# An SSD chunk loop with its products turned over: diagonal and skip on VectorE, gate on GpSimd, features kept transposed

## The chip, the cores and the metric

One core of one Trainium2 chip. The metric is the device time of one execution in microseconds (us). Times below are of single executions; the median is over three.

## The reference

Two layers over 1024 latent rows and 256 context rows, width 1024: windowed attention, then a bidirectional Mamba-2 SSD mixer, and a final RMSNorm. The change lies in the mixer. Per group of heads (8 groups of 4 heads of 64, state size 128) and per chunk of 128 rows it needs, cut to what matters:

```
a_cs   = cumsum(dt * A)                        # per head, forward or backward
states = einsum(B, exp(a_last - a_cs), x*dt)   # one state per chunk, then a scan over chunks
cb     = einsum('bcqgn,bcsgn->bcqsg', C, B)
y_diag = einsum(cb, exp(a_cs[q]-a_cs[s]) where s<=q, x*dt)
y_off  = einsum(C, h_prev, exp(a_cs))
y      = y_f + y_b + d_skip * x                # both directions, and the skip
u      = rms_normalize(y * silu(z))            # over the 256 columns of a group
out    = (u * norm_w) @ w_out
```

The latent scans start from the states that the context rows leave behind.

## The kernel before, in words

All large products run in split form: an f32 operand is taken apart into a high and a low part (hi is a cast, lo the difference), and three products hi*hi, hi*lo, lo*hi are summed in PSUM. The small products of the SSD part run in plain f32, each of which shows in the trace as two passes.

Attention comes first (up to about 690 us), then its output projection and the set-up of the decay rates (`dt_setup`, `dt_chain`, L914 to L1029). `ssd` (L1193) then loops over the 8 groups. For each group `front` (L1048) makes, in this order, B (tile bT), two halves of x, C (cT) and the gate z: projections on TensorE (L1143 for the context's 256 rows, L1152 for the 1024 latent rows, L1177 for z), a 5-tap convolution (`taps`, L1038 on VectorE), a silu, and transposes back to natural layout (`natural`, L1085, L1088). In L1177 the 128 rows of a chunk are stationary and 256 columns of the weight move, so that z comes out with rows on partitions; L1185 and L1188 make its silu.

`states` (L1223) walks the context's four chunk states and then the backward ones of the latent chunks: a weighting on GpSimd (L1213), a product (L1236), a decay on GpSimd (L1218) and a sum on VectorE (L1248). It is a generator, and `tick` advances it by one step, three times per chunk, once the group's x is finished; what is left runs at the end of the group.

`slot` (L1276) does one chunk of the current group, and between its steps `fill` runs pieces of the next group's `front`:

- L1282 makes C.B for the chunk (tile pcb), L1284 and L1285 the products with the forward and backward states (po: rows on partitions, two directions of 256 columns);
- L1286 multiplies the decays M, four heads of 128x128, with pcb; L1290 to L1293 advance the forward state (L1291 on TensorE);
- L1295 scales po by exp(a_cs), a per-row factor from the table `eacs`;
- L1300 takes the diagonal of pcb, L1302 makes the per-row skip factor sk, L1306 multiplies x by it on GpSimd, L1307 and L1308 sum the parts on GpSimd;
- L1311 is the diagonal product, four heads, M stationary and x moving with 64 columns; L1320 adds it, L1321 multiplies by the gate (both VectorE);
- L1323 squares and sums along the row (ScalarE), L1324 makes the power -1/2 (GpSimd), L1329 scales the row (ScalarE);
- `decays` (L1267) makes M for the next chunk: L1265 on GpSimd, L1270 on VectorE, four exponentials L1272 on ScalarE; `load_rows` (L1257) loads its rows two chunks ahead;
- the tail, run in the next chunk, transposes y twice (L1341), multiplies by norm_w on eviction (L1342) and stores the features (L1343).

During the last group `ssd_out` (L1433) runs instead of a front: it loads the features back (L1517), casts and splits them (L1529, L1526), casts and splits the weights (L1503, L1507) and runs the output projection (L1571, later L223 to L225).

Order: instructions are emitted by these generators under a planner (`Queue`, L64): FRONT and OUT are the planned costs of a front and of the output projection, SEGS the shares of the fill in a chunk. A scheduler then orders each engine's instructions along a simulated timeline, so that the emitted order is a priority. Each engine, and SyncE's DMA queue, then works in the order that it was given. PSUM has eight banks: pj2 (two tiles of two banks) for the projections, psX (three) for the slot's products, psD (one) for context and states.

## Time and profile before

| | us |
|---|---|
| median of three (1813.79, 1818.71, 1822.03) | 1818.71 |
| the profiled execution | 1818.37 |
| its span, first to last instruction | 1816.6 |
| start of the first chunk, and of the last group's first chunk | 857.2, 1593.9 |
| last product of the output projection's sweeps (L1571) | 1749.0 |

The page of the profile gives the busy time of each engine, with matmul ends that are modelled: TensorE's times overlap, so spacing between starts is the better price. The profile's other views used here are: stages (busy time per engine in a stretch of time), groups of instructions (count, busy sum, mean of one, idle time before), waits (who waited for whom: total, times, longest), the chain (the work that ended last), and the timeline of single instructions. PE is TensorE, DVE is VectorE, ACT is ScalarE, POOL is GpSimd, SP is SyncE, and SPq is its DMA queue.

### The profile page before, as it was taken

What the parts mean: (1) busy time and instruction counts of PE and PEld (TensorE: products, weight loads), DVE (VectorE), ACT (ScalarE), POOL (GpSimd) and SP (SyncE); (2) the same over time, 40 slices, a digit from 0 to 9 for tenths busy, and PEclk for the clock granted to TensorE, in tenths of its full rate; (3) what the DMA queues carried; (4) which work ended last, traced back from release to release, by engine and by line L of the source; (5) the groups of instructions that cost most, each with busy time, mean ns of one, the idle gap of its engine ahead of it and who ended that gap; (6) DMA issues with size and microseconds to landing.
All of it is one profiled execution on the core that took longest, in us unless ns stands there. A gap on an engine that the chain in (4) does not pass through costs nothing.

```text
span 1816.6 us, 29129 instructions
## 1 busy us (share of the span) xinstructions
PE 1749.0 (96%) x10379; PEld 1500.2 (83%) x10379; DVE 1166.0 (64%) x2125; ACT 869.9 (48%) x1895; POOL 811.1 (45%) x1074
## 2 busy tenths in 40 slices
PE   6999998999999899999999999999999999999997
PEld 3797767788889687778898898989889898988886
DVE  3563536786787766675766748567675857766643
ACT  3521235677788766352444434344353434544522
POOL 2441127554456465303454544646454454644311
PEclk9999999999999999999999999999999999999998
DMA  8768865543345445311322323323332322655542
GB/s 296 285 156 255 261 192 138 119 116 99 99 117 132 118 133 195 112 42 52 86 68 79 93 69 88 82 71 79 78 93 78 82 79 74 188 163 179 163 137 70
DMA packets 209393, 227.89 MB, mean 125 GB/s; under 512 B 16096, under 2 KB 149088, under 8 KB 208224
## 3 DMA queue, kind: packets, MB, share of 16 engines
q1 hardware_dynamic: 175184, 207.38, 38.1%
q0 software_dynamic: 34064, 18.65, 5.6%
q8 instruction: 82, 1.34, 0.3%
q14 instruction: 63, 0.52, 0.1%
HBM read 191.14 MB, written 35.13 MB: 125 GB/s over the span
## 4 chain that ended last, share of the span: by engine, by line
PE 83%; DVE 5%; ACT 4%; DMA 4%; issue 3%; POOL 0%; SPq 0%; DVEq 0%; ACTq 0%; POOLq 0%
PE pj L1152 17%; PE pj L1177 10%; PE pj L1571 7%; PE pj L223 6%; PE pj L225 6%; PE pj L224 6%; PE psD L1143 3%; PE pt L694 3%; PE psX L1311 2%; PE pv L701 2%; PE psD L1236 2%; PE pv L700 2%; PE S L669 2%; PE psX L1285 1%; PE S L670 1%
## 5 line engine op out<-in xcount | busy, mean ns | idle before, releaser
L223 PE MATMUL pj<-uH,wh 128*128 128x256 f32 (+1 forms) x652 | 233.5, 358 | 8.1 <-DVE rope_b L532 2.3
L224 PE MATMUL pj<-uL,wh 128*128 128x256 f32 (+1 forms) x652 | 220.1, 338 | 0.0
L225 PE MATMUL pj<-uH,wl 128*128 128x256 f32 (+1 forms) x652 | 220.1, 338 | 0.0
L211 POOL TENSOR_TENSOR wl<-wr,wh 128x512 fp32r<-128x512 f32 x92 | 121.7, 1326 | 97.4 <-ACT wh L209 96.9
L1152 PE MATMUL pj<-uH,wh 128*128 128x512 f32 x480 | 161.4, 410 | 2.0 <-ACT xn L1088 1.2
L1152 PE MATMUL pj<-uH,wl 128*128 128x512 f32 x480 | 158.5, 403 | 0.0
L1152 PE MATMUL pj<-uL,wh 128*128 128x512 f32 x480 | 157.3, 402 | 0.0
L699 DVE TENSOR_TENSOR pl<-pt,ph 128x512 fp32r<-128x512 f32 x168 | 114.2, 687 | 61.3 <-ACT ph L698 60.4
L223 PEld LDWEIGHTS pj<-uH,wh 128*128 128x128 f32 x652 | 124.7, 191 | 34.9 <-issue 8.6
L1177 PE MATMUL pj<-wh,uH 128*128 128x256 f32 x512 | 148.0, 289 | 3.1 <-ACT xn L1088 3.0
L1177 PE MATMUL pj<-wl,uH 128*128 128x256 f32 x512 | 150.7, 294 | 0.0
L1213 POOL TENSOR_TENSOR xw<-xn,dtdec 128x256 f32<-128x256 f32 x144 | 92.9, 649 | 127.1 <-PE psD L1236 108.5
L1177 PE MATMUL pj<-wh,uL 128*128 128x256 f32 x512 | 149.5, 292 | 0.0
L1342 ACT ACTIVATE uT<-psX,nw 128x128 f32<-128x128 f32 x128 | 46.7, 365 | 193.2 <-PE psX L1341 193.1
L225 PEld LDWEIGHTS pj<-uH,wl 128*128 128x128 f32 x652 | 124.4, 191 | 14.8 <-issue 1.7
L673 DVE CUSTOM_DVE_ANT_0 sm<-S,mask,nsink 128x640 f32<-128x640 f32 (+2 forms) x160 | 118.7, 772 | 26.5 <-PE S L670 14.5
L224 PEld LDWEIGHTS pj<-uL,wh 128*128 128x128 f32 x652 | 124.9, 192 | 11.5 <-issue 2.8
L209 ACT CAST wh<-wr 128x512 fp32r<-128x512 f32 (+1 forms) x132 | 84.8, 645 | 102.5 <-PE pj L224 78.7
L698 ACT CAST ph<-pt 128x512 fp32r<-128x512 f32 x168 | 97.5, 585 | 64.5 <-PE pt L694 58.9
L675 ACT ACTIVATE sm<-sm,nm 128x640 f32<-128x640 f32 (+2 forms) x160 | 118.5, 742 | 12.6 <-DVE nm L673 12.3
L1152 PEld LDWEIGHTS pj<-uL,wh 128*128 128x128 f32 x480 | 90.1, 188 | 19.0
L1152 PEld LDWEIGHTS pj<-uH,wh 128*128 128x128 f32 x480 | 89.1, 188 | 19.6 <-ACT bn L1088 2.0
(383 smaller groups left out, 4999.8 us busy)
## 6 DMA issues: line engine op xcount, KB each, us to landing
fd<-acs SPq DMA_DIRECT2D x64, 256.0 KB, 5.0
bd<-acs SPq DMA_DIRECT2D x64, 256.0 KB, 5.2
wr<-w_x SPq DMA_DIRECT2D x31, 512.0 KB, 3.8
wr<-w_sk SPq DMA_DIRECT2D x24, 512.0 KB, 4.0
wr<-wg SPq DMA_DIRECT2D x44, 256.0 KB, 4.6
qs<-q POOLq DMA_DIRECT2D x40, 256.0 KB, 3.9
wr<-wo SPq DMA_DIRECT2D x40, 256.0 KB, 2.7
wada<-w_ad SPq DMA_DIRECT2D x8, 1024.0 KB, 6.4
```

What stands on the lines that cost most here:

```text
L211: (eng or nc.vector).tensor_tensor(l, raw, h, op=ALU.subtract)
L223: self.nc.tensor.matmul(ps, lh, rh, start=first and i == 0, stop=False)
L224: self.nc.tensor.matmul(ps, lh, rl, start=False, stop=False)
L225: self.nc.tensor.matmul(ps, ll, rh, start=False, stop=last and i == n - 1)
L673: nc.vector.tensor_tensor_reduce(out=sm[:, :W], in0=Sv, in1=self.mask[:, m0 : m0 + W], scale=-SCALE, scalar=self.nsink[:, 4 * j + r : 4 * ...
L675: nc.scalar.activation(sm[:, :W], sm[:, :W], AF.Exp, bias=nm[:, r : r + 1], scale=-1.0, accum_out=sums[:, r : r + 1])
L698: nc.scalar.copy(ph, ptf)
L699: nc.vector.tensor_sub(pl, ptf, ph)
L1152: nc.tensor.matmul(raw[:, 512 * i : 512 * i + 512], l[:, k, :], r[i][:, k, :], start=k + y == 0, stop=k == KT - 1 and y == 2)
L1177: nc.tensor.matmul(pj[:, c], l, r[:, k, :], start=c % 2 + q + k + y == 0, stop=c % 2 == 1 and q == 1 and k == 3 and y == 2)
L1213: nc.gpsimd.tensor_tensor(xw, X(st, c).rearrange("p (r h) -> p r h", r=R), self.dtdec[:, c, hd(d, g)].unsqueeze(2).broadcast_to([P, R, HP] ...
L1571: nc.tensor.matmul(banks[x], l[:, z, sl], r, start=k == 2 * qs[0] and y == 0, stop=k == 2 * qs[-1] + 1 and y == 2)
```

## The change

The chunk's output is made with columns on partitions, so that it is already in the layout of the output projection:

- z is projected with the weight stationary and 512 rows moving (96 products of 512 columns per group for 192 of 256);
- the states are stationary and C moves: four products of 128 columns for two of 256; exp(a_cs) now varies along the free axis, so its rows are written to DRAM once (sixteen stores in `dt_chain`) and loaded for each chunk by two broadcast loads (`load_scale`), two chunks ahead;
- the skip goes into M's diagonal: L1300 and L1302 stay, then four multiply-adds with the identity on VectorE, one per head, before the diagonal product;
- the diagonal product has x stationary (64 columns) and M moving (128 columns); its two heads of a pair write partitions 0 to 63 and 64 to 127;
- the product with the gate moves from VectorE to GpSimd, and the result is stored at once; the two transposes and their evictions go;
- the squares' sum is a product with a column of ones in the tail; the power is taken once for four chunks, and its rows go through DRAM (`rn_d`); the output projection loads them by broadcast, multiplies each feature tile by them on GpSimd, and takes norm_w into the cast and the split;
- `tick` runs four times per chunk, and four steps of the next group's states may run as soon as its context part of x is there;
- FRONT and SEGS follow: more fill ahead of the diagonal.

```diff
-FRONT = 4 * 48 * N512 + 3 * 24 * N256 + 8 * 24 * N256
+FRONT = 4 * 48 * N512 + 3 * 24 * N256 + 4 * 24 * N512
-SEGS = (1.5, 2.0, 2.0, 2.2, 2.2)
+SEGS = (3.0, 1.6, 1.8, 1.8, 1.8)
...
         nc.scalar.activation(acs, acs, AF.Exp)
+        for d in range(2):
+            for f in range(2):
+                for r in range(R):
+                    row = 64 * d + 32 * f + r
+                    nc.sync.dma_start(self.eacs_d[r % 2, :, d, r // 2, 512 * f : 512 * f + 512], acs[row : row + 29 : 4, :512])
...
+                if kind == 1:
+                    post.append((LATE, [lambda: st.__setitem__("early", 4)]))
...
-                for c in range(4):
-                    for k in range(4):
-                        u, v = uH[i][:, 4 * q + k, c * P : (c + 1) * P], uL[i][:, 4 * q + k, c * P : (c + 1) * P]
-                        for y, (l, r) in enumerate(((u, ww["h"]), (u, ww["l"]), (v, ww["h"]))):
-                            nc.tensor.matmul(pj[:, c], l, r[:, k, :], start=c % 2 + q + k + y == 0, stop=c % 2 == 1 and q == 1 and k == 3 and y == 2)
+                for k in range(KT):
+                    for y, (l, u) in enumerate(((ww["h"], uH), (ww["h"], uL), (ww["l"], uH))):
+                        nc.tensor.matmul(pj[:, q], l[:, k, :], u[i][:, k, :], start=k + y == 0, stop=k == KT - 1 and y == 2)
...
+        def load_scale(n):
+            if n < G * NCH:
+                g, c = divmod(n, NCH)
+                x = eb[n] = t(ps2, [P, 2, 2, P], F32, "eb")
+                for f in range(2):
+                    src = self.eacs_d[f : f + 1, g, :, :, c * P : (c + 1) * P].rearrange("o d e q -> o (d e) q")
+                    nc.sync.dma_start(x[64 * f : 64 * f + 64].rearrange("p d e q -> p (d e) q"), src.broadcast_to([64, R, P]))
...
-            nc.tensor.matmul(po[:, :256], st["cT"][:, cs], flat(st["hf"]), start=True, stop=True)
-            nc.tensor.matmul(po[:, 256:], st["cT"][:, cs], flat(st["hb"][c]), start=True, stop=True)
+            for d, h in enumerate((st["hf"], st["hb"][c])):
+                for e in range(2):
+                    nc.tensor.matmul(po[:, d, e], flat(h)[:, e * P : (e + 1) * P], st["cT"][:, cs], start=True, stop=True)
...
+            for r in range(R):
+                nc.vector.scalar_tensor_tensor(M[:, r], in0=self.ident, scalar=sk[:, r : r + 1], in1=M[:, r], op0=ALU.mult, op1=ALU.add)
+            nc.vector.tensor_tensor(y2, po, x, op=ALU.mult)
             fill(0)
-            nc.gpsimd.tensor_tensor(xs, xc, sk.unsqueeze(2).broadcast_to([P, R, HP]), op=ALU.mult)
-            nc.gpsimd.tensor_tensor(yv, y2[:, 0], y2[:, 1], op=ALU.add)
-            yadd = nc.gpsimd.tensor_tensor(yv, yv, xs, op=ALU.add)
+            yadd = nc.gpsimd.tensor_tensor(y, y2[:, 0], y2[:, 1], op=ALU.add)
+            load_scale(n + 2)
             yd = t(ps, [P, 512], F32, "psX")
             for r in range(R):
-                nc.tensor.matmul(yd[:, r * HP : (r + 1) * HP], M[:, r], X(st, c)[:, r * HP : (r + 1) * HP], start=True, stop=True)
+                e, f = divmod(r, 2)
+                nc.tensor.matmul(yd[64 * f : 64 * f + 64, e * P : (e + 1) * P], X(st, c)[:, r * HP : (r + 1) * HP], M[:, r], start=True, stop=True)
...
-            ymul = nc.vector.tensor_mul(yf, yf, st["sz"][c])
-            nc.scalar.activation(y2.rearrange("p d r h -> p (d r h)")[:, :257], y[:, :257], AF.Square, scale=1.0 / 16.0, accum_out=ss)
-            nc.gpsimd.tensor_tensor(ss, ss, self.half, op=ALU.pow)
+            ymul = nc.vector.tensor_add(y, y, yd[:, :256].rearrange("p (e q) -> p e q", e=2))
+            nc.gpsimd.tensor_tensor(y, y, st["sz"][c], op=ALU.mult)
+            nc.sync.dma_start(self.uN_d[g][:, :, cs].rearrange("e p n -> p e n"), y)
+            nc.scalar.activation(y2[:, 0], y, AF.Square, scale=1.0 / 16.0)
+            nc.gpsimd.tensor_tensor(sq, y2[:, 0, 0], y2[:, 0, 1], op=ALU.add)
...
-                for e in range(2):
-                    nc.tensor.transpose(pt[:, e * P : (e + 1) * P], yf[:, e * P : (e + 1) * P], self.ident)
-                    nc.scalar.activation(uT[:, e], pt[:, e * P : (e + 1) * P], AF.Copy, scale=self.nw[:, 2 * g + e : 2 * g + e + 1])
+                nc.tensor.matmul(pt[:, :1], sq, self.ones[:, :1], start=True, stop=True)
+                nc.scalar.activation(ss[:, c % 4 : c % 4 + 1], pt[:, :1], AF.Identity, bias=self.eps4)
+                if c % 4 == 3:
+                    nc.gpsimd.tensor_tensor(ss, ss, self.mhalf, op=ALU.pow)
+                    nc.sync.dma_start(self.rn_d[g][c // 4].rearrange("o (c p) -> p (o c)", c=4), ss)
...
-                    if g < G - 1 and 1 in nst:
+                    if 1 in nst or nst.get("early"):
...
+                def scale():
+                    nc.gpsimd.tensor_tensor(feats[n], feats[n], scales[k // 2 % 2][:, k // 4 % 2 * 512 :][:, :512], op=ALU.mult)
```

More of the change, by code (lines that the diff above doesn't have):

```diff
@@ L1196, in ssd @@
         self.uN_d = [t(self.dr, [2, P, P * NCH], F32, f"uN{g}") for g in range(G)]
+        self.rn_d = [[t(self.dr, [1, 512], F32, f"rn{g}_{i}") for i in range(2)] for g in range(G)]
         self.wp = self.pool("ws", ctx=c0)
@@ L1301, in slot @@
[L1301 to L1308 removed]
+            x = eb.pop(n)
@@ new lines, in slot @@
+            y2 = t(ps2, [P, 2, 2, P], F32, "y2")
+            sk = t(ps2, [P, R + 1], F32, "sk")
+            dg, sk = sk[:, R:], sk[:, :R]
+            nc.vector.tensor_tensor_reduce(out=y2[:, 0, 0], in0=pcb, in1=self.ident, scale=1.0, scalar=0.0, op0=ALU.mult, op1=ALU.add, accum_out=dg)
+            nc.vector.scalar_tensor_tensor(sk, in0=self.dtb[:, c, 4 * g : 4 * g + 4], scalar=dg, in1=self.dsk[:, 4 * g : 4 * g + 4], op0=ALU.mult, op1=ALU.add)
+            for r in range(R):
+                nc.vector.scalar_tensor_tensor(M[:, r], in0=self.ident, scalar=sk[:, r : r + 1], in1=M[:, r], op0=ALU.mult, op1=ALU.add)
```

76 lines of the change are left out of this document (35 added, 41 removed).

## The prediction

> **What bounds the kernel now.** I read the page first (busy time, chain), then the stages, then what TensorE waits for inside the slot loop, then single instructions.
>
> ```profile
> PE 1749.0 (96%) x10379; PEld 1500.2 (83%) x10379; DVE 1166.0 (64%) x2125; ACT 869.9 (48%) x1895; POOL 811.1 (45%) x1074
> PE 83%; DVE 5%; ACT 4%; DMA 4%; issue 3%; POOL 0%; SPq 0%; DVEq 0%; ACTq 0%; POOLq 0%
> ```
>
> TensorE is busy for 96% of the span and carries 83% of the chain that ended last. The changed part is the loop over groups and chunks. One row of it, the third group's 105.5 us, and the last group's stage (busy us per engine, instruction counts in brackets):
>
> ```profile
> 1066.60:1172.10 105.50, 104.75 (x652) 93.75 (x651) 71.96 (x123) 45.34 (x105) 53.63 (x75) 1.00 0.29 77
> 1593.90:1700.00 106.10, 105.89 (x514) 87.75 (x513) 66.08 (x113) 49.60 (x108) 45.65 (x57) 1.00 0.57 174
> ```
>
> In a group TensorE is idle for 0.75 us, VectorE for 34, GpSimd for 52, ScalarE for 60. All that TensorE waited for between 857 and 1593.9 us, in the loop's first seven groups:
>
> ```profile
> PE pj L1177 <- ACT xn L1088: 2.1, 6, 0.3
> PE pj L1085 <- ACT xn L1088: 1.6, 6, 0.3
> ```
>
> That is 3.7 us in 737. So in this stage time is TensorE's own work: work taken from TensorE shortens the kernel one for one, work added to it lengthens it, and what moves between the other engines costs nothing until TensorE has to wait for it. The parts below are therefore counted in TensorE time first, and then in the cover that the others have.
>
> Busy sums overlap (a matmul's modelled end lies after the next one's start), so I take prices from start to start. The profiled execution is the base: span 1816.6, time 1818.4, against a median of 1818.7; the difference of 0.3 is nothing.
>
> **Term 1, the gate projection (L1177) in 512-wide products.** Before, each group issues 192 products of 256 columns, 1536 in all; after, 96 of 512, 768 in all. Two pieces of the chain give the price of each kind:
>
> ```profile
> 1070.62 5.04 PE pj L1152 x22
> 1167.70 3.23 PE pj L1177 x27
> ```
>
> 512 columns cost 5.04/22 = 0.229 us, 256 columns 3.23/27 = 0.120. 1536 x 0.120 = 184; 768 x 0.229 = 176. Gain 8 us. Its tanh and product (L1185, L1188) keep their size.
>
> **Term 2, the diagonal products (L1311), which change sides.** Before: four f32 products per chunk, M stationary, x moving with 64 columns; each is two passes.
>
> ```profile
> 1127.16 1.00 PE L1311 MATMUL psX<-xn,fd 128*128 128x64 f32 x8
> 1127.97 0.48 PE L1152 MATMUL pj<-uL,wh 128*128 128x512 f32 x1
> ```
>
> Start to start 0.81 us for eight passes, 0.10 each. What the columns themselves cost is seen in the state product:
>
> ```profile
> 1075.93 0.59 PE L1291 MATMUL psX<-xw,bn 128*128 128x256 f32 x2
> 1076.36 1.00 PE L1311 MATMUL psX<-xn,fd 128*128 128x64 f32 x8
> ```
>
> Two passes of 256 columns take 0.43, so 0.215 a pass, and 128 columns would take 0.108: no more than the 0.10 that 64 columns take now. So turning the product over doubles its columns at no loss. After, x is stationary with 64 columns, and the two heads of a pair write output partitions 0 to 63 and 64 to 127. Do the two then run at once? The kernel has one place that writes strips, the modulation (L187): four 32-column products into four strips, two passes each, 512 columns.
>
> ```profile
> 152.38 0.28 PE L225 MATMUL pj<-uH,wl 128*128 128x256 f32 x1
> 152.59 1.07 PE L187 MATMUL aps<-wh,cs 128*32 128x512 f32 x8
> 153.59 0.50 PE L223 MATMUL pj<-uH,wh 128*128 128x512 f32 x1
> ```
>
> Eight passes in 1.00 us, where one after another would take 8 x 0.43 = 3.4. The strips run together: two rounds of 0.43, and 0.14 left over on leaving; on entering, 152.38 to 152.59 is 0.21 where a 256-column product takes 0.12, so 0.09 more. If halves pack as quarters do, a chunk's diagonal is four rounds of 0.108 = 0.43, plus up to 0.23 for going in and out. A 64-column product elsewhere shows nothing on entry:
>
> ```profile
> 765.73 0.39 PE L1114 MATMUL pj<-uH,wfh 128*128 128x512 f32 x1
> 765.96 0.39 PE L942 MATMUL psX<-uH,wdth 128*64 128x512 f32 x1
> ```
>
> 0.23 as between full products (but it is alone in its half, so it says nothing about packing). I take the middle, 0.43 + 0.12 = 0.55: gain 0.26 a chunk, 64 x 0.26 = 17 us. Ends: no switching cost, 0.43, gain 24; full switching cost, 0.66, gain 10; no packing, 8 x 0.108 = 0.86, loss 3; neither packing nor a free switch, 1.09, loss 18.
>
> The Trainium skill, "TensorEngine Tiling (Array Packing)", Key Properties under Tiling Modes, says that a change of tiling mode drains TensorE, which speaks against two changes of mode per chunk. The strips' 0.09 and 0.14 agree with it. By that rule the gain of this term would be the 10 us, and the whole would come out at the first rival's time below.
>
> **Term 3, transposes out, a sum over partitions in.** Before, a chunk transposes y twice (L1341); after, one f32 product with one column sums the squares.
>
> ```profile
> 1694.62 0.39 PE L1571 MATMUL pj<-uH,wl 128*128 128x512 f32 x1
> 1694.85 0.27 PE L1341 MATMUL psX<-ident,y 128*128 128x128 f32 x1
> 1694.88 0.48 PE L1571 MATMUL pj<-uH,wh 128*128 128x512 f32 x1
> 1695.19 0.39 PE L1571 MATMUL pj<-uL,wh 128*128 128x512 f32 x1
> ```
>
> 1694.62 to 1695.19 is 0.57 with two 512-column products of 0.229 in it: a transpose costs 0.11, two 0.22.
>
> ```profile
> 1715.74 0.40 PE L1571 MATMUL pj<-uH,wl 128*128 128x512 f32 x1
> 1715.97 0.28 PE L344 MATMUL psX<-ones,xn 128*128 128x1 f32 x2
> 1716.11 0.48 PE L1571 MATMUL pj<-uH,wh 128*128 128x512 f32 x1
> 1716.43 0.40 PE L1571 MATMUL pj<-uL,wh 128*128 128x512 f32 x1
> ```
>
> 0.69 less 0.46: 0.23 for the one-column product. Net 0. The inter-chunk product (L1284, L1285) goes from two of 256 columns to four of 128: 4 x 0.215 = 8 x 0.108, net 0. Four transposes less in the setup: 0.4 us, left out.
>
> **The other engines, and their cover.** VectorE gains four 128-column multiply-adds per chunk (the diagonal) and loses the gate's product:
>
> ```profile
> L1302 DVE SCALAR_TENSOR_TENSOR sk<-dtb,dg,dsk 128x4 f32<-128x4 f32 x8 | 1.7, 215 | 0.0
> L1038 DVE SCALAR_TENSOR_TENSOR cctx<-psD,cw,cctx 128x254 f32<-128x254 f32 (+1 forms) x12 | 5.7, 471 | 0.0
> L1321 DVE TENSOR_TENSOR y<-y,sz 128x256 f32<-128x256 f32 x8 | 4.3, 540 | 0.2
> ```
>
> 128 columns lie between the 4-column 0.215 and the 254-column 0.471; I take 0.3, so 4 x 0.3 - 0.54 = 0.66 a chunk, 5 us a group: 72 becomes 77 of about 103. GpSimd loses two sums and most of a power, and gains the gate's product and a 128-column sum; ScalarE loses two evictions (0.365 each) and a scaling, and gains a one-column copy:
>
> ```profile
> L1308 POOL TENSOR_TENSOR y<-y,xs 128x256 f32<-128x256 f32 x8 | 5.9, 735 | 0.4
> L1324 POOL TENSOR_TENSOR ss<-ss,half 128x1 f32<-128x1 f32 x8 | 4.6, 578 | 12.0 <-ACT y L1323 12.0
> L1342 ACT ACTIVATE uT<-psX,nw 128x128 f32<-128x128 f32 x16 | 5.8, 365 | 27.1 <-PE psX L1341 27.1
> ```
>
> Both end lower. In the output stage GpSimd gains 32 products of 512 columns, 1.59 us each by its own sums there:
>
> ```profile
> L1471 POOL TENSOR_TENSOR xn<-xn,bn 128x512 f32<-128x512 f32 x7 | 11.1, 1589 | 9.4 <-ACT bn L1470 8.9
> ```
>
> 51 us, spread over the 154 us in which L1571 runs (below), beside the 46 of its own up to 1700: it fits. The features now wait for one more chain (a power, an element-wise write, a broadcast read, a product). What hides it:
>
> ```profile
> L1526 DVE TENSOR_TENSOR uL<-oraw,uH x32: 676/688/1781, 1579.7 to 1717.8; 128x512 fp32r<-128x512 f32 x32
> L1571 PE MATMUL pj<-uH,wh x192: 387/389/587, 1594.9 to 1749.0; 128*128 128x512 f32 x192
> ```
>
> The last feature is split at 1717.8 and TensorE works on such products until 1749. Without those 31 us the chain would cost about two DMAs and two GpSimd steps, some 10 us, once.
>
> SyncE issues two more loads a chunk, behind which weights and rows queue. A load's issue and landing:
>
> ```profile
> 1077.39 0.36 SPq L1261 DMA_DIRECT2D fd<-acs  x1
> fd<-acs SPq DMA_DIRECT2D x64, 256.0 KB, 5.0
> ```
>
> Sixteen more at 0.36 are 6 us of a group's 105 in that queue; each waits for the scaling (L1295) of two chunks ago and is due a chunk later. I cost it at nothing. Starting the next group's states from the context on moves pool products and state products forward inside the group; TensorE's count stays, and only the 3.7 us of waits could shrink.
>
> **The added wait.** M now needs the skip column before L1311 may start, and behind L1311 in TensorE's queue stand the projections. Two chunks of the group:
>
> ```profile
> 1121.39 0.22 DVE L1302 SCALAR_TENSOR_TENSOR sk<-dtb,dg,dsk 128x4 f32<-128x4 f32 x1
> 1104.33 0.21 DVE L1302 SCALAR_TENSOR_TENSOR sk<-dtb,dg,dsk 128x4 f32<-128x4 f32 x1
> 1103.16 1.00 PE L1311 MATMUL psX<-xn,fd 128*128 128x64 f32 x8
> ```
>
> In the one, the column is ready at 1121.61 and L1311 starts at 1127.16: 5.5 us of cover for 1.2 us of multiply-adds. In the other, L1311 started at 1103.16, 1.4 us before the column was ready, so in today's order it would come 2.6 us late. The order is made anew, with 3.0 of 10 shares of projection ahead of the diagonal (1.5 of 9.9 now). I leave 4 us in all for such waits, between 0 (all reordered) and 21 (2.6 once in each group).
>
> **The sum.** -8 (gate) -17 (diagonal) +0 (transposes) +4 (waits) = -21: 1818.4 to 1797.4, say 1798.
>
> **The rivals.**
> *Packed, with the strips' full switching cost.* -8 -10 +4 = -14: 1804. For it, the strip rows; against it, the 64-column product entering free.
> *No packing.* The halves run one after another: -8 +3 +4 = -1: 1817; with a switching cost on top 1832. For it: no row shows two halves at once. Against it: quarters do run at once.
> *VectorE's diagonal holds TensorE back (slower).* In-order TensorE stands before L1311 until the four multiply-adds are done. 2.6 us each time; from (25 + 9)/2.6 = 13 chunks of 64 on, it is slower by over 0.5%. With two late chunks in each of eight groups: 16 x 2.6 = 42, -25 + 42 = +17: 1835. For it: the chunk at 1103. Against it: 34 us a group in which VectorE is idle, and a schedule free to put projections between.
> *Everything pays.* Packed, free switching, no waits: -8 -24 = -32, and the 3.7 us of waits gone: 1783.
>
> **How the numbers follow.** About 0.5% (9 us) is what a measurement of this kernel can tell from no change: 1810 to 1828. Forecast 0.40, full switching cost 0.20, everything pays 0.10, no packing 0.15 (0.02 of it with a switching cost), VectorE late 0.08, other waits that I have not found 0.07 (0.05 of them about as large as the gain, 0.02 larger). The first three are faster, 0.70; no packing with a free switch and the waits as large as the gain are the same, 0.13 + 0.05 = 0.18; the rest is slower, 0.02 + 0.08 + 0.02 = 0.12. The range from 1779 to 1820 holds the first three with their bounds and no packing with a free switch, and leaves out no packing with a switching cost, VectorE late and the larger losses.
>
> **What would show it.** Right: in a chunk, eight passes of the diagonal in 0.43 to 0.66 us start to start; the gate's products 0.229 apart; groups of about 102.5 us instead of 105.5; TensorE's waits in the slot loop still a few us. Wrong: diagonal passes 0.108 apart one by one; TensorE waiting for VectorE's M at the diagonal, or for GpSimd's scaled features in the output stage.

## The result, and the profile after

The changed kernel takes 1917.23 us (median of 4 runs, 1914.28 to 1919.13) where the kernel before takes 1818.9 (median of 4): a ratio of 1.0542, 95% interval 1.0514 to 1.057. It is 98 us slower, where 21 us less were forecast. The profiled execution has a span of 1915.8 us.

First the page of the changed kernel: busy time, and the chain that ended last.

```profile
PE 1789.3 (93%) x9863; PEld 1462.0 (76%) x9863; DVE 1266.7 (66%) x2315; ACT 814.9 (43%) x1699; POOL 837.4 (44%) x1058
...
PE 2%; DVE 0%; ACT 0%; DVEq 0%; issue 0%
```

TensorE issues 516 matmuls less and is busy 40 us longer. Its share falls from 96% to 93%: the span grew by 99 us, so some 59 of them are new idle time. The chain says nothing here, since it could be followed back over a few per cent of the span only; stages must be read instead. The third group and the two halves of the last stage (busy us per engine, instructions in brackets, then TensorE's granted clock, DMA share, GB/s):

```profile
1085.40:1197.10 111.70, 108.03 (x589) 88.40 (x588) 83.95 (x155) 38.09 (x81) 54.26 (x72) 0.97 0.38 97
1638.80:1740.00 101.20, 87.85 (x415) 66.79 (x413) 68.47 (x120) 33.39 (x67) 63.35 (x67) 0.93 0.69 186
1740.00:1850.00 110.00, 93.34 (x399) 74.08 (x398) 60.52 (x72) 38.20 (x60) 46.03 (x36) 0.91 0.50 131
```

The group's 105.50 us became 111.70, with 3.7 us of idle TensorE instead of 0.75. In the last stage TensorE is idle for 30 of 211 us and its clock is 0.92 on average, where before it was full at 1.00. Of the idle time, 11 us lie before 1710 us and 17 between 1730 and 1790. I measure by the start of the gate's last product of each group: in before these lie at 857.1, 961.0, 1066.5 ... 1593.7 us, every 105.5 after a first step of 103.9; after at 857.3, 958.7, 1085.4 ... 1638.8, in steps of 101.3, 126.7, 111.8, 112.8, 107.6, 112.1, 109.2. So 45 us are lost in the loop, 21 of them in its second group. From there to the output's last product before takes 155.7 us and the changed kernel 209.8: 54 us more. The two make the 99 us between the two spans. Of the 54, 30 are idle time and 24 busy time. At a clock of 0.92 the 155.6 us for which TensorE was busy there before would take 169 (an estimate, the one divided by the other), so the lower clock accounts for some 14 of the 24; the other 10 are not traced.

What TensorE waited for in the loop (the first four rows, of 32 us of idle time in all, where before it waited for 3.7), and in the last stage:

```profile
PE psD L1240 <- DVE hb L1252: 8.9, 9, 2.2
PE psD L1240 <- POOL xw L1217: 4.4, 2, 2.2
PE pj L1158 <- ACT xn L1092: 3.7, 3, 1.3
PE psX L1299 <- DVE hb L1252: 3.5, 2, 1.8
...
PE psX L1324 <- DVE fd L1315: 9.8, 10, 2.3
PE psX L1299 <- ACT ss L1357: 9.3, 1, 9.3
PE pj L1596 <- ACT uH L1548: 2.9, 2, 1.8
```

The states (L1240) head the list of the loop, and the diagonal does not appear in it. In the last stage the diagonal's wait for the multiply-adds (L1315) heads the list; what the removal of the multiply-adds gives is measured below. Who holds ScalarE in the last stage shows one level further back, in ScalarE's own waits up to 1780 us:

```profile
ACT uH L1548 <- POOL oraw L1545: 45.4, 16, 15.1
```

Sixteen feature casts waited for GpSimd's scaling, one of them for 15.1 us, and whatever stood behind them in ScalarE's queue waited too, the eviction of the squares (L1357) among it. That longest wait can be followed from queue to queue, in the timelines of SyncE's DMA queue, GpSimd, ScalarE and TensorE:

```profile
1736.84 0.36 SPq L1360 DMA_DIRECT2D rn<-ss  x1
1745.47 0.33 SPq L1533 DMA_DIRECT2D cT<-rn  x1
1751.03 2.48 POOL L1545 TENSOR_TENSOR oraw<-oraw,cT 128x512 f32<-128x512 f32 x2 [13.79 <-DMA cT<-rn]
1752.32 0.72 ACT L1548 ACTIVATE uH<-oraw,nw 128x512 fp32r<-128x512 f32 x1 [15.10 <-POOL oraw L1545]
1755.11 0.25 ACT L1357 ACTIVATE ss<-psX,eps 128x1 f32<-128x1 f32 x1
1755.41 1.22 PE L1299 MATMUL psX<-cT,hf 128*128 128x128 f32 x4 [9.34 <-ACT ss L1357]
```

The factors of the last group's first four chunks are stored at 1736.84. Their load can go only when the store has landed, 8.2 us later; then come the load, the product, the cast and, behind the cast, the eviction, and TensorE has been idle for 9.34 us.

Of the forecast's four signs of being right, two came out as drawn, an unbroken diagonal and the gate's price; groups of 102.5 us and waits of a few us did not. Both signs of being wrong by waiting came out too, in the last stage: TensorE waiting for the multiply-adds, and for what stood behind the scaled features. The diagonal, unbroken and broken by the order:

```profile
1120.17 0.27 PE L1089 MATMUL pj<-ident,bT 128*128 128x128 f32 x1
1120.37 0.66 PE L1324 MATMUL psX<-fd,xn 128*64 128x128 f32 x8
1120.96 0.38 PE L1353 MATMUL psX<-ones,sq 128*128 128x1 f32 x2
...
1128.77 0.43 PE L1324 MATMUL psX<-fd,xn 128*64 128x128 f32 x2
1129.13 0.39 PE L1147 MATMUL psD<-uH,wh 128*128 128x256 f32 x1
...
1129.68 0.43 PE L1324 MATMUL psX<-fd,xn 128*64 128x128 f32 x2
1130.04 0.39 PE L1147 MATMUL psD<-uH,wh 128*128 128x256 f32 x1
1130.36 0.44 PE L1324 MATMUL psX<-fd,xn 128*64 128x128 f32 x4
```

Eight passes in 0.59 us from start to start, against 0.81 before and 0.86 for eight of 128 columns one by one: the halves do run together. On entry a transpose of 0.11 takes 0.20, so 0.09 more. But the second visit is in three pieces, and each pays for going in and out again; two passes take 0.36 where a quarter of 0.59 is 0.15. Counted by their starts, there are 95 such visits for 64 chunks. The gate's products are 0.23 apart:

```profile
1170.44 0.40 PE L1180 MATMUL pj<-uL,wh 128*128 128x512 f32 x1
1170.67 0.40 PE L1180 MATMUL pj<-uH,wl 128*128 128x512 f32 x1
1170.90 0.40 PE L1180 MATMUL pj<-uH,wh 128*128 128x512 f32 x1
```

### The profile page after: what moved, and what is told of

Its sections match the earlier page's. It is cut to its first block, busy times and chain, and to the rows that moved or that the text cites. A ratio compares the mean times of both kernels' runs of the same rounds, so it can differ in the third digit from the quotient of the medians.

```text
span 1915.8 us, 28419 instructions
## 1 busy us (share of the span) xinstructions
PE 1789.3 (93%) x9863; PEld 1462.0 (76%) x9863; DVE 1266.7 (66%) x2315; ACT 814.9 (43%) x1699; POOL 837.4 (44%) x1058
## 5 line engine op out<-in xcount | busy, mean ns | idle before, releaser
L1158 PE MATMUL pj<-uH,wh 128*128 128x512 f32 x480 | 158.3, 408 | 6.6 <-ACT xn L1092 3.7
L1335 POOL TENSOR_TENSOR yt<-yt,sz 128x256 f32<-128x256 f32 x64 | 70.0, 1094 | 115.0 <-DVE yt L1334 92.0
L1315 DVE SCALAR_TENSOR_TENSOR fd<-ident,sk,fd 128x128 f32<-128x128 f32 x256 | 115.5, 510 | 0.6
L1286 ACT ACTIVATE fd<-fd,vf 128x128 f32<-128x128 f32 x256 | 81.9, 392 | 66.9 <-DVE fd L1284 66.8
L1180 PE MATMUL pj<-uH,wh 128*128 128x512 f32 x256 | 103.2, 403 | 4.5 <-ACT xn L1092 3.6
```

Source lines behind the costliest of these rows:

```text
L1158: nc.tensor.matmul(raw[:, 512 * i : 512 * i + 512], l[:, k, :], r[i][:, k, :], start=k + y == 0, stop=k == KT - 1 and y == 2)
L1180: nc.tensor.matmul(pj[:, q], l[:, k, :], u[i][:, k, :], start=k + y == 0, stop=k == KT - 1 and y == 2)
L1315: nc.vector.scalar_tensor_tensor(M[:, r], in0=self.ident, scalar=sk[:, r : r + 1], in1=M[:, r], op0=ALU.mult, op1=ALU.add)
```

## The experiments

Numbers are medians of four runs or more where an interval or a spread is given, and one run otherwise; loops, stages and groups are those of the one profiled execution. The kernel before took 1812.6 to 1818.1 us beside them. I give the "loop" (start of the last gate product of the last group, 1593.7 in before, 1638.8 after) and the "last stage" (from there to the output's last product, 155.7 and 209.8).

### First round: the chain of a chunk, the diagonal, the scaling, the early states

**The scratch.** VectorE's diagonal sum (L1312) writes its unused product into y2, which the squares of the chunk before still hold. Here it goes into the free part of its PSUM bank.

```diff
-out=y2[:, 0, 0], in0=pcb, in1=self.ident
+out=pcx[:, P : 2 * P], in0=pcb, in1=self.ident
```

> One edit to the changed kernel: the read-out of pcb's diagonal (L1312) puts its unused product into the free part of pcb's own PSUM bank, not into y2, of which there is one buffer. Theory A (the chunks are chained: chunk n+1's read-out, and with it the skip, the diagonal and everything after, waits for chunk n's sum of squares, L1339, the last reader of y2): the chain opens, and the time falls by most of the 98 us lost, to 1795 to 1830. Theory B (VectorE is late with the four multiply-adds): unchanged, 1905 to 1925. Theory C (the early states crowd psD) and theory D (GpSimd's scaling of the features holds the last stage): unchanged or within 10 us.

1916.97 us (1909.72 to 1921.45), ratio to before 1.0577 (1.0553 to 1.06). No effect on the time. In the changed kernel VectorE waited 20.9 us for the squares at this instruction; here it no longer does, and the next product into y2, which needs the same buffer, waits for them for 1.9 us. So that chain was there, and it did not hold the kernel.

**The states late.** The next group's states start when its second x tile is done, as in before, with three ticks a chunk.

```diff
-post.append((LATE, [lambda: st.__setitem__("early", 4)]))
+pass
...
-            tick()
```

> The changed kernel with the next group's states started as before: no early steps, three ticks a chunk. Theory C: the waits of the state products for VectorE (L1240 on L1252) go, and the groups come back to about 105 us: 1860 to 1880. Theory A: the chain stays, 1905 to 1930.

1888.22 us: 29 of the 98 go. Loop 1611.3, last stage 209.6; the groups are even now, 106.6 us each, with one of 112.1. The early start alone, on the kernel before:

> One part alone in the kernel before: four steps of the next group's states from its context on, and four ticks a chunk. If early states by themselves crowd TensorE's order: 1835 to 1850. If they only hurt together with the longer chunk of the changed kernel: 1810 to 1825.

1823.79 us beside 1812.56 (and 1816 to 1819 on other chips); its groups take 105.6 us. The early start costs 5 to 11 us by itself and 29 in the changed kernel: what it costs depends on what else is there (single runs, both).

**No diagonal on VectorE.** The four multiply-adds (L1315) are dropped, so the skip and the backward diagonal are missing.

```diff
-            for r in range(R):
-                nc.vector.scalar_tensor_tensor(M[:, r], in0=self.ident, scalar=sk[:, r : r + 1], ...)
```

> The changed kernel without the four multiply-adds on VectorE (L1315), so that the skip and the backward diagonal are left out of the output. Theory B: TensorE no longer waits for them, and most of the loss goes: 1810 to 1840. Theory A: the chain from pcb to the sum of squares gets 2 us shorter in each of 64 chunks, of which the schedule hides a part: 1860 to 1900.

1901.7 us, 15 less; loop 1621.5, last stage 211.3. All of it lies in the loop: the 9.8 us for which TensorE waited for the multiply-adds in the last stage gave nothing back there.

**The scaling on VectorE** (`nc.gpsimd` to `nc.vector` in the feature's product):

> The changed kernel with the 32 products that scale the features put on VectorE instead of GpSimd. Theory D: the last stage gives back most of its 54 us: 1865 to 1885. Theory A: GpSimd's links of the chain come sooner in the last stage, but the chain stays: 1885 to 1915.

1917.72 us, nothing gained. VectorE now stands where GpSimd stood: in its queue the products wait 29.5 us for features and 17.1 for factors. So the engine that scales is not what the stage hangs on, but what the scaling waits for.

### Second round, on the kernel with the states late

**No scaling.** No product, no load of factors; the output is not normalised per group.

> The changed kernel with the states late (as in the run that took 1888), and with the features' scale left out: no loads of its rows and no products L1545, so that the output is not normalised per group. Theory D2 (the last stage loses its 53 us because every feature must wait for the scale's rows, whose buffers come free only when group 6 ends, and for a product on GpSimd): the first output product comes right after the last front again, and the time is 1835 to 1850. Rival (the last stage is slow from the chunks' own chain, pcb to the sum of squares): 1875 to 1890.

1868.74 us, 19 less. The factors are still stored here. What is left in the last stage shows in ScalarE's timeline:

```profile
1597.49 0.37 ACT L1092 COPY xn<-psD 128x256 f32<-128x256 f32 x1 [0.79 <-PE psD L1089]
1612.02 1.33 ACT L1545 ACTIVATE uH<-oraw,nw 128x512 fp32r<-128x512 f32 x2 [14.15 <-DMA oraw<-uN]
```

ScalarE stands 14.15 us at a feature that has not landed. All 16 DMA engines are busy meanwhile and move little; two stretches of the same kernel:

```profile
1596.00:1600.00 4.00, 4.00 (x24) 3.45 (x23) 3.81 (x10) 1.08 (x2) 1.53 (x3) 1.00 0.87 244
1600.00:1607.00 7.00, 7.00 (x39) 5.51 (x38) 0.79 (x2) 0.00 (x0) 2.93 (x4) 1.00 1.01 42
```

The second begins 3 us after the store of a group's factors (L1359, 512 elements of 4 bytes, issued at 1596.75): 42 GB/s at a share of 1.01.

**Factors in other buffers**, free from the middle of the group before (`"xn4"` for `"bT"` and `"cT"`):

> States late, and the scale's rows in the buffers of group 6's x (the tag xn4) instead of its B and C, used half by half, so that the first four features can be scaled from the middle of group 6 on. If the late buffers are the cause of the last stage's loss: 1850 to 1870. If it is the product on GpSimd in the middle of the chunks' work: 1880 to 1890.

1887.64 us, no change: late buffers are not what delays the factors.

**The heads in another order**, 0, 2, 1, 3, so that neighbours in the program lie in the same half. It was meant to take packing away:

```diff
-            for r in range(R):
+            for r in (0, 2, 1, 3):
```

> States late, and the four heads of the diagonal product issued in the order 0, 2, 1, 3, so that neighbours write the same half and can hardly run at once. If packing is worth what the prediction took (0.26 us a chunk, 17 us), the eight passes take 0.9 to 1.0 us instead of 0.59 and the time is 1900 to 1910. If the switches eat it: within 6 us of 1888.

1903.12 us, 15 more; its groups take 109.2 us instead of 106.6. The time is the one foreseen, and the reason is another. A whole diagonal still runs two halves at once, and four passes of two heads of one half do not:

```profile
911.64 0.67 PE L1324 MATMUL psX<-fd,xn 128*64 128x128 f32 x8
912.24 0.38 PE L1352 MATMUL psX<-ones,sq 128*128 128x1 f32 x2
...
1015.37 0.65 PE L1324 MATMUL psX<-fd,xn 128*64 128x128 f32 x4
1015.95 0.38 PE L1295 MATMUL psX<-cT,bT 128*128 128x128 f32 x1
```

Eight passes take 0.60 us, not the 0.9 to 1.0 expected; four of two heads that lie in one half by the program's order take 0.58, where four of two halves take 0.37. What the new order of heads changed most is how often the diagonal is cut: 120 visits instead of 90, and 58.6 us for the 64 chunks instead of 48.6. So this run prices cuts, 10 of its 15 us; it does not take packing away, and what packing is worth in all was not measured.

### Third round: the store of the factors

**Not stored at all**, on top of no scaling:

> The kernel with the states started late and no per-group scaling (1868.7 us), and the factors of the normalisation not stored either (nothing reads them there). The output is not normalised per group. Seen in its trace: in the 5 to 7 us after each of the 16 stores of 512 elements of 4 bytes, the DMA engines move mostly under 50 GB/s, and behind the one at 1596.7 us the issue of the next four loads takes 10.24 us, ScalarE stands 14.2 us at the first feature, and the states' evictions stand behind that. Theory S (the element-wise stores hold the DMA engines, and rows, scalings and features behind them come late): the time falls by 15 to 40 us, to 1830 to 1855, the first feature lands about 10 us earlier, and TensorE's clock stays at 1.00 in the first 40 us of the last stage. Theory Q (the order of casts and evictions in ScalarE's and VectorE's queues is the cause, whatever the stores do): 1864 to 1869.

1856.2 us (1855.78 to 1859.0): 12.5 less than the single run above, below the 15 to 40 that the theory claimed, and the clock fell to 0.57 between 1620 and 1640 us where 1.00 was expected.

**Stored in 128 pieces of 16 bytes**, the scaling reading with a stride; first with the states late, then in the changed kernel itself:

```diff
-self.rn_d[g][c // 4].rearrange("o (c p) -> p (o c)", c=4)
+self.rn_d[g][c // 4].rearrange("o (p c) -> p (o c)", c=4)
```

> The kernel with the states started late (1888.2 us), and the factors stored in the order in which they stand in SBUF, 128 pieces of 16 bytes instead of 512 of 4; the scaling reads them with a stride instead. The same values are computed. Theory S, if a store's price goes by its pieces: three quarters of what f1_late_nostore gains, so 1858 to 1877, and the lull behind each store shrinks from 5 to 7 us to 1 to 2. Theory Q: 1885 to 1891; or slower, if GpSimd's product with the stride is longer than its 1.6 us.

> The changed kernel (1917.2 us) with the factors stored in 128 pieces of 16 bytes, and read with a stride by the scaling. The same values are computed. Theory S: 10 to 30 us less, 1887 to 1907, and the loop's groups even out, since the rows and scalings behind a store come in time. Theory Q: 1914 to 1920.

1885.9 us (1883.03 to 1889.49) and 1908.4 (1905.58 to 1912.37): 2 and 9 less. The lull itself is gone. In the first of the two kernels, whose store is issued at 1594.63:

```profile
1595.00:1602.00 7.00, 7.00 (x43) 5.60 (x41) 4.21 (x8) 1.69 (x3) 4.02 (x6) 1.00 0.86 259
```

259 GB/s where it was 42. The lull is real, but by itself it was at most a tenth of the loss.

### Fourth round: the gate's width, and the bank

By now the place of the loss was known and its origin not. The states show it. In before, states of the first group and, from 1383.1 us on (the end of the gate), the last states of a group and the first context product of the next:

```profile
833.61 0.59 PE L1236 MATMUL psD<-xw,bn 128*128 128x256 f32 x2
...
837.63 0.59 PE L1236 MATMUL psD<-xw,bn 128*128 128x256 f32 x2
...
1392.10 0.59 PE L1236 MATMUL psD<-xw,bn 128*128 128x256 f32 x2
...
1397.11 0.47 PE L1143 MATMUL psD<-uH,wh 128*128 128x256 f32 x1
```

The changed kernel's first group:

```profile
843.64 0.59 PE L1240 MATMUL psD<-xw,bn 128*128 128x256 f32 x2
...
849.11 0.59 PE L1240 MATMUL psD<-xw,bn 128*128 128x256 f32 x2
```

And the kernel with the states late, whose gate ends at 1398.0 us:

```profile
1430.39 0.70 PE L1240 MATMUL psD<-xw,bn 128*128 128x256 f32 x2 [0.58 <-DVE hb L1252]
...
1432.90 0.36 PE L1147 MATMUL psD<-uH,wh 128*128 128x256 f32 x1
```

In before, the first group's states come 3.3 to 4.3 us apart beside a gate of 256 columns; after, 5.5 us apart beside one of 512, nearly without waiting: so they were ordered. Context and states share the one psD bank. In before the last state comes 9 us after the gate, and the next context product 14 us after it; with the states late these are 32 and 35, and in the changed kernel the context comes 23 to 33 us after the gate. The context is then late, the states that need it are late again, and with the states late nine of a group's eleven stand behind the gate instead of two. In the last group no projections of a next group are left to stand between them.

**The gate in 256 columns again**, still turned over, with the planner's prices to match (FRONT and the cost of a product) and nothing else changed; then with the states late; then the first with the factors stored in 16-byte pieces:

```diff
-                for k in range(KT):
+                for v in range(2):
+                    for k in range(KT):
...
-                        nc.tensor.matmul(pj[:, q], l[:, k, :], u[i][:, k, :], ...)
+                            nc.tensor.matmul(pj[:, q, 256 * v : 256 * v + 256], l[:, k, :], u[i][:, k, 256 * v : 256 * v + 256], ...)
```

> The changed kernel with its gate projection in 256 columns again (still turned over: twice as many products, 8 us more TensorE time by the prediction's prices), nothing else. Why it might matter: in the changed kernel the states of a group are issued late. In before the last of them come 9 us after the gate's last product of their group, and the next group's first context product at 14 us; with the states started late in the changed kernel these are 32 and 35 us. Context and states share the one psD bank, so late states push the next group's context back, which pushes its states back. In the order in which TensorE's instructions stand in the built program, products of 256 columns bring the states of the first group 3.5 to 4 us apart instead of 5, and all states of a later group before its gate ends; the output product then starts 1 us after the gate. Theory Z (the wide gate products move the states in the order, and the rest follows through psD): 1795 to 1830, groups of 104 to 105, output product within 160 us. Theory Q (the longer chain of a chunk over VectorE, GpSimd and ScalarE and the scaling of features are the cause): 1917 + 8 = 1920 to 1928.

> The same with the states started late as in before (the kernel of 1888.2 us with the gate in 256 columns). Theory Z: 1795 to 1830; against g1_z256 it says what the early start is worth when the order is not disturbed: within 10 us. Theory Q: 1890 to 1898.

> g1_z256 with the factors stored in 128 pieces of 16 bytes. Theory Z with the stores' lull a second, smaller cost: 0 to 10 us under g1_z256. If the lull costs nothing once the states are in time: within 3 us of it.

1874.79 us (1871.15 to 1881.95, ratio 1.0316, 1.0279 to 1.0353), 1868.38 (1864.82 to 1871.74) and 1864.47 (1862.52 to 1866.78). Undoing the one part that was booked as a clear gain takes 42 us off the changed kernel, though TensorE has more to do. In the first group its states stand where they stood in before, 3.3 to 4.3 us apart, from the second group on they are done before the gate ends, the context follows 1.5 to 3 us behind the gate, and the groups take 107.4 us; loop 1614.6, last stage 195.9. That is neither of the two answers foreseen: Theory Z has its direction and not its size. Late states now differ from early ones by 6 us, not 29. The store is worth 10 here, and it is the last stage that it shortens, to 180.6 in the profiled execution.

**Two psD banks** (and two psX instead of three), gate in 512 columns, states late:

```diff
-... pj2=2, psX=3, sk=2, dg=2,
+... pj2=2, psX=2, psD=2, sk=2, dg=2,
```

> The kernel with the states started late (1888.2 us), gate in 512 columns as changed, but two psD banks and two psX banks instead of one and three: context and states no longer wait for one another's bank. In the order of the program the states then start at 70 us of a group instead of 92, and 5 instead of 9 are left after the gate. If psD is what couples the groups: 1830 to 1870, with the last stage shorter by 15 us or more. If not, or if the chunk's own products now wait for a psX bank: 1880 to 1910.

1869.2 us (1863.69 to 1874.63), 19 less than with one bank. From the second group on the context comes 7 to 16 us after the gate instead of 35, and the loop ends at 1596.3, 2.6 us from before's; the last stage stays long, 203.4. So psD carries the delay from group to group, and the last stage has a cause of its own.

### Fifth round: the rest

**No scaling, with the order mended**, in both ways; nothing is loaded or stored of the factors, and the output is not normalised per group:

> g1_z256 (1874.8 us) without the per-group scaling: no product, no load of factors, and the factors not stored. Its output is not normalised per group. In g1_z256 the loop ends 21 us later than in before, and from the gate's last product to the output's last it takes 195.9 us where before takes 155.7. Theory R (the round trip of the factors: store, load, a product of 1.6 us on GpSimd ahead of each feature's cast, and ScalarE's queue behind the cast): the last stage falls to 155 to 165, so 1834 to 1844. Rival (in the last stage ScalarE, VectorE and GpSimd are late whatever is scaled, by the chunk's own longer chain): 1855 to 1870.

> g4_late_banks (1869.2 us; gate in 512 columns, states late, two banks each for psD and psX) without the per-group scaling in the same way; its output is not normalised per group. Its last stage takes 203.4 us and its loop ends only 2.6 us later than before's. Theory R: 1821 to 1835, no slower than before by more than 1%. Rival: 1845 to 1865.

1849.65 us (1848.05 to 1850.48) and 1837.85 (1835.01 to 1842.0): 25 and 31 less; last stage 195.9 to 166.1, and 203.4 to 171.7. The first lies midway between the two theories and the second nearer to R. By the last stage the round trip of the factors, their store included, holds most of what there was: 30 of the 40 us over before in the one kernel, 32 of 48 in the other.

**And without the multiply-adds on VectorE**, on the first of the two:

> The kernel with the gate in 256 columns and no per-group scaling (1849.7 us), without the four multiply-adds on the diagonal (0.51 us each, 2.0 a chunk) that stand between the last write of M and the diagonal's products; the skip and the backward diagonal are missing from its output, besides the normalisation. The order of TensorE's instructions stays nearly the same. Its groups take 107.4 us, of them 6.8 in the diagonal's products, where before takes 6.4 and the packed passes alone would be 4.7. Theory V (TensorE stands at pieces of a split diagonal until the next head's multiply-add is done): the diagonal falls to about 5 us a group, groups to 105.5, the whole to 1830 to 1838. Rival (the splits and switches come of the order, not of VectorE): 1844 to 1850, the diagonal still 6 to 7 us a group.

1832.56 us (1830.79 to 1835.56), 17 less, in the range of Theory V. Groups take 106.3 us instead of 107.4, the diagonal 5.1 us of them instead of 6.8. Over the 64 chunks the diagonal falls from 56.6 to 39.7 us, which is the whole 17. Only 3.6 us of that were waits for the multiply-adds, and there Theory V was wrong: for the rest TensorE did not stand at them. With them the diagonal is cut into 115 visits, without them into 70; that the order cuts it because the heads come ready one after another is argued, not shown.

TensorE's time in one group by kind of product, each from its start to the next one's start, so with the wait behind it, and below it the diagonal of all 64 chunks (us; the last column's groups are uneven, 104.4 to 107.8, and this is one of the shortest):

| | before | states late | heads 0, 2, 1, 3 | gate 256, no scaling | the same, no multiply-adds | two banks, no scaling |
|---|---|---|---|---|---|---|
| projections | 46.7 | 46.8 | 47.3 | 45.9 | 46.3 | 46.4 |
| gate | 24.9 | 22.9 | 23.0 | 24.5 | 24.7 | 23.8 |
| context, its and other transposes | 12.3 | 12.4 | 12.4 | 12.0 | 12.1 | 12.5 |
| states | 3.5 | 5.6 | 5.4 | 4.5 | 3.1 | 4.1 |
| inter-chunk | 5.7 | 7.0 | 6.7 | 6.8 | 8.9 | 6.7 |
| diagonal | 6.4 | 5.7 | 7.5 | 6.8 | 5.1 | 4.9 |
| B'C, chunk states, y transposes or squares | 6.0 | 6.3 | 6.9 | 7.0 | 6.2 | 6.1 |
| group | 105.5 | 106.6 | 109.2 | 107.4 | 106.3 | 104.4 |
| diagonal, 64 chunks | 51.9 | 48.6 | 58.6 | 56.6 | 39.7 | 45.7 |
| its visits | 88 | 90 | 120 | 115 | 70 | 70 |

In the changed kernel itself the diagonal takes 58.3 us in 95 visits, and 43.4 in 70 without the multiply-adds.

One path from the changed kernel back to before, each step measured on top of the one above it:

| step | us | change |
|---|---|---|
| the changed kernel | 1917.2 | |
| gate in 256 columns | 1874.8 | -42 |
| factors stored in 16-byte pieces | 1864.5 | -10 |
| no scaling, no factors at all | 1849.7 | -15 |
| no multiply-adds on VectorE | 1832.6 | -17 |
| the kernel before, same runs | 1816.9 | -16 |

The first two steps compute the same as before; 1864.5 is the best kernel of this study that does, and it does not beat the kernel before, so no version with both layouts' merits is offered. The last 16 us are not traced: 9 lie in the loop, whose groups there wait 12.2 us in all for the natural tiles on ScalarE (L1092), and 6 in the last stage, at 161.8 us. Nor does a trace show why products of 512 columns make the schedule place states further apart; that they do is seen in two kernels that differ in nothing but the gate's width and the planner's prices for it.

## Why the prediction was wrong, step by step

**The base step.** "What moves between the other engines costs nothing until TensorE has to wait for it" was right as a sentence, and the order of TensorE's queue was left out of it. 0.75 us of idle in a group was taken as a property of the work; it was one of the order in which states, context and gate stood. This is the step that failed first: a new place of the states in that order was put at nothing, and the gate in 256 columns, which mends it, gave 42 of the 98 us back. Two more steps failed, the cover of the multiply-adds (15 to 17 us) and the round trip of the factors (25 with its store), both below.

**Term 1, the gate, -8: the price held, and what came with it failed.** 0.23 a product was measured as forecast, and with the states late a group's gate fell from 24.9 to 22.9 us, twice the forecast 1.0 a group. What came with it was not priced: the states' place in the order. Undone, it gave back 42 us, though a group's gate then takes 24.5 again. In the profiled executions 24 of the gain lie in the loop and 14 in the last stage.

**Term 2, the diagonal, -17: right by the visit, wrong in sum.** A whole visit takes 0.59 us, 0.55 forecast, with the halves running at once. The Trainium skill, "TensorEngine Tiling (Array Packing)", Key Properties, has a change of mode drain TensorE, and the trace agrees, with 0.09 on entry. But the 64 chunks take 58.3 us in the changed kernel and 48.6 with the states late, where before took 51.9: 6 more or 3 less, not 17 less. The sum paid the change of mode once a chunk. It is paid at every visit, and there are 95 for 64 chunks, since the schedule put other work between the heads. Visits were cut in before too, 88 of them, and there it cost little:

```profile
1149.19 0.33 PE L1311 MATMUL psX<-xn,fd 128*128 128x64 f32 x2
1149.36 0.65 PE L1236 MATMUL psD<-xw,bn 128*128 128x256 f32 x2
```

Two passes take 0.17 here and 0.36 after. Where the order leaves most visits whole, 70 of them, the gain over before is 12 us (no scaling, no multiply-adds) and 6 us (two banks, no scaling).

**Term 3: right for transposes against squares** (2.3 us a group against 1.9 to 2.3), **not for the inter-chunk product**: four of 128 columns for two of 256 were called equal, and the row of the table goes from 5.7 to between 6.7 and 7.0 in four of the kernels, and to 8.9 in one. That is 1.0 to 1.3 us a group, 8 to 10 in all.

**VectorE, +0.66 a chunk, covered: wrong twice.** The multiply-add costs 0.51 on average, not 0.3, and a group's VectorE time rose from 72.0 to 84.0 us, not to 77:

```profile
L1315 DVE SCALAR_TENSOR_TENSOR fd<-ident,sk,fd 128x128 f32<-128x128 f32 x256 | 115.5, 510 | 0.6
```

Two chunks of the changed kernel, first VectorE, then GpSimd in the first of them:

```profile
1223.49 2.39 DVE L1315 SCALAR_TENSOR_TENSOR fd<-ident,sk,fd 128x128 f32<-128x128 f32 x4
...
1232.93 1.14 DVE L1315 SCALAR_TENSOR_TENSOR fd<-ident,sk,fd 128x128 f32<-128x128 f32 x4
```

```profile
1223.64 0.78 POOL L1319 TENSOR_TENSOR yt<-y 128x256 f32<-128x256 f32 x1 [4.02 <-DVE y L1316]
1224.38 1.09 POOL L1279 TENSOR_TENSOR bd<-bd,vo 128x512 f32<-128x512 f32 x1
```

Beside GpSimd the four take 2.39 us; in the other chunk, where GpSimd starts nothing until the fourth, 1.14. Of the 256 multiply-adds, 146 overlap GpSimd's instructions by less than 0.05 us and take 0.343 on average (0.353 at most), 110 overlap them by more and take 0.731. The Trainium skill, "SBUF — State Buffer", in its section on the two separate sides, has VectorE with two SBUF inputs and GpSimd take turns at one pair of ports; this trace agrees. And idle time elsewhere in the group was no cover, because these stand between M and the diagonal: 15 to 17 us by their removal, and the diagonal alone gets shorter by as much. Against the allowance of 4 for the added wait, the rival "VectorE's diagonal holds TensorE back" had 0.08 and was right in its place. Its mechanism held in part: in the loop of the changed kernel TensorE does not wait for the multiply-adds, and the diagonal is cut more often with them (95 visits) than without (70). Its 42 us were too many, and as the whole loss it is a sixth.

**The output stage, "it fits", "covered by 31 us": failed.** Removing the scaling gave 19 us with the store of the factors kept, and 25 and 31 in two kernels without it. GpSimd had the time: 1.45 us a product (1.35 and 1.56 on average in its two groups of 16). The chain did not: store, load and product stand ahead of each cast, and the evictions of the squares stand behind the casts in ScalarE's queue. The 31 us lay at the stage's end; the idle time lies ahead of it, where the first features are due at once and where the last group's own factors come back. The forecast put the whole chain, without that cover, at two DMAs and two GpSimd steps, some 10 us, once; the store shown above alone held back the load behind it for 8.2 us.

**SyncE's 16 more loads, at nothing: open.** The DMA share over the loop went from 0.34 to 0.43 with the states late; no run took these loads away.

**"TensorE's count stays" for the early states: the count did.** The fourth tick and the early start cost 29 us with the gate at 512 columns and 6 at 256.

No rival named the order, and the range ended at 1820: nearly all of its working priced work and waits in the order of before.

## What to carry to other kernels

Where a scheduler orders the queues anew, price the order too: look up which bank, buffer or queue couples the next stage's early steps to this stage's late ones (here one psD bank), and how far those late steps are from it. Cover has a place: it counts at the point where the new wait stands, not as idle time of the stage. A long chain that goes through an in-order queue charges everything behind it, so a cast should not be queued ahead of evictions until its input is there. And a price that is paid on going in and out is counted by visits, not by units of work: look up in the profile of before how often the schedule cuts the work.

## What the runs showed of the hardware

- Behind a store of 512 elements of 4 bytes the DMA engines were busy and moved little (42 GB/s at a share of 1.01 for 7 us); behind the same 2 KB in 128 pieces of 16 bytes they moved 259 GB/s.
- Two products into the two halves of the output partitions run together: 8 passes of 128 columns in 0.59 us, 4 in 0.37 from two halves and 0.58 from one, and 2 alone in 0.36.
- A VectorE multiply-add of 128 x 128 with both inputs in SBUF took 0.343 us alone and 0.731 on average beside GpSimd; GpSimd's product of 128 x 256 with the gate takes 1.094 on average, where the sum over the same size took 0.735 in before.
- TensorE's granted clock fell after a stretch with idle time, in the kernel with the states late and neither scaling nor store: 1.00 in a 20 us stretch in which it was busy for 16.4, 0.57 in the next, in which it was busy for 15.0, and 1.00 again in the one after, which was full.
